# A four-layer trunk in split-float32 products: gate tiles and most of the conv input projection as seven half-width products per pair of weight tiles

## The chip, the cores and the metric

The kernel runs on one core of one Trainium2 chip. The metric is the device time of one execution in microseconds. One launch computes the whole network; the inputs come from HBM and the result goes back to HBM. The names of the engines are those of the profile: PE (TensorE) with its weight loads PEld, DVE (VectorE), ACT (ScalarE), POOL (GpSimd), SP (SyncE, which issues most DMAs).

## The reference

One sequence of 512 tokens with 1024 features goes through four layers, pool, conv, MLA, pool, and a last norm. Each layer is `x = x + mixer(rms_norm(x))`; everything is float32 and D_INNER is 2048. The pool mixer's `pooled` is the trailing mean over 2, 4, 8 or 16 tokens minus the token; MLA's `o` comes from 16 heads of causal softmax attention.

```python
def pool_mixer(xn, w_in, w_grp, scale, w_out):
    u, z = jnp.split(xn @ w_in, 2, axis=-1)            # 1024 -> 2 x 2048
    ...
    mixed = jnp.einsum('bsgc,gcd->bsgd', pooled, w_grp).reshape(B, S, D_INNER) * scale
    return (mixed * jax.nn.silu(z)) @ w_out            # 2048 -> 1024

def conv_mixer(xn, w_in, conv_w, w_out):
    b, c, h, z = jnp.split(xn @ w_in, 4, axis=-1)      # 1024 -> 4 x 2048
    y = b * causal_depthwise_conv(c * h, conv_w)       # width 3
    return (y * jax.nn.silu(z)) @ w_out

def mla_mixer(...):
    q_lat, kv_lat, k_rope, z = jnp.split(xn @ w_in, [384, 640, 704], axis=-1)   # z has 2048
    ...
    return (o.reshape(B, S, D_INNER) * jax.nn.silu(z)) @ w_out
```

## The kernel before

Activations lie feature-major: a tile is 128 features by 512 tokens, so `x` is 8 tiles and an inner activation is 16. Weights arrive from HBM in chunks of 128x1024 (512 KB): the 8 k-tiles of 128x128 that make one output tile of an input projection, or half of one of an output projection.

A float32 product is made of three faster products. Each operand is split into a high part (rounded, type fp32r) and a low part (the rest), and `mm3` (L156 to L159) adds high by high (L157), high by low (L158, here with the activation's low part) and low by high (L159). A weight chunk goes through `wchunk`: one DMA on SP, the high part `wh` on ACT (L152), the low part `wl` on DVE (L153). `mtile` runs the 8 k-tiles of one output tile through `mm3`: 24 matmuls of 128x512 into one PSUM bank. The activations are split once per layer (`xh` L230, `xl` L231), unnormed; the norm's factor of each token comes later (`Stats`, L175 to L218) and is multiplied into each output tile as `R`.

The stages in order of time are: pool layer 0 (to about 225 us of the profile), its output projection (to 315), the conv layer's input projection (to 690) and output projection (to 765), the MLA layer's input projection (to 885), its attention (to 1097), output projection (to 1185), pool layer 1 with its output projection and the closing norm (to 1505). In the input projections a `Layer` runs tile after tile. What is done with an output tile is its post: in pool, `post_u` scales it and makes sliding sums on POOL, `post_z` scales the gate tile (`sz`, L280) and applies SiLU; in conv, a channel tile takes four output tiles: c and h are multiplied (`post_c`, `post_h`), three taps make the convolution (L360 to L362), b is multiplied in on DVE and `R` on POOL (`post_b`, L366 and L367), and the gate z, then the product is split (`post_z`, L373 and L139); in MLA, sixteen gate tiles are among the first tiles' and the attention's work.

No order is written down for the engines, apart from a few `issue_after` hints: a scheduler places each instruction when its program is built, from its own estimates. Tiles of activations share one pool of 67 buffers, chunks have their own pools.

Of the kernel before, what the change touches and what calls it, by code (L numbers as in the profile page):

```python
# [33 lines left out]
CH = 1024  # L34
WARM = 8
# [7 lines left out]
# columns of the per-partition parameter array  # L43
# [11 lines left out]
# columns of the constant array  # L55
# [4 lines left out]
def trunk_kernel(ctx: ExitStack, tc: tile.TileContext, a):  # L60
    nc = tc.nc
    cp = ctx.enter_context(tc.tile_pool(name="cp", bufs=1))
    xp = ctx.enter_context(tc.tile_pool(name="xp", bufs=1))
    wp = ctx.enter_context(tc.tile_pool(name="wp", bufs=3))
    up = ctx.enter_context(tc.tile_pool(name="up", bufs=67))
# [11 lines left out]

    def ps(s):
        return pp.tile([P, S], F32, tag="ps", name=nm(s))
# [5 lines left out]
    con = cp.tile([P, NCON], F32, name="con")  # L85
    par = cp.tile([P, NPAR], F32, name="par")
    xt = [xp.tile([P, S], F32, name=f"x{m}") for m in range(KD)]
    dummy = cp.tile([P, S], F32R, name="dummy")
# [10 lines left out]

    raw0 = {}  # L100
# [4 lines left out]
    def load_w(m, hf):  # L105
        raw0[m, hf] = ut("wr")
        nc.sync.dma_start(raw0[m, hf], a["pool_in0"][m][:, hf * S : (hf + 1) * S])
# [11 lines left out]
    raw2 = []  # L119
    for m in (2, 3):  # L120
        raw2.append(wp.tile([P, CH], F32, tag="wr", name=nm("wr")))
        nc.sync.dma_start(raw2[-1], a["pool_in0"][m])
    nc.sync.dma_start(con, a["con"])
# [5 lines left out]
    def pcol(name, i):  # L129
        return par[:, PC[name][0] + i : PC[name][0] + i + 1]  # L130

# [10 lines left out]
    def wchunk(src, width=CH, pool=False, raw=None):  # L142
        if raw is None:
            raw = wp.tile([P, CH], F32, tag="wr", name=nm("wr"))[:, :width]
            nc.sync.dma_start(raw, src)
        h = wp.tile([P, CH], F32R, tag="wh", name=nm("wh"))[:, :width]
        l = wp.tile([P, CH], F32R, tag="wl", name=nm("wl"))[:, :width]
        if pool:
            nc.gpsimd.tensor_scalar(out=h, in0=raw, scalar1=1.0, scalar2=1.0, op0=ALU.mult, op1=ALU.mult)
            nc.gpsimd.tensor_tensor(out=l, in0=raw, in1=f(h), op=ALU.subtract)  # L150
        else:
            nc.scalar.activation(h, raw, AF.Copy)  # L152
            nc.vector.tensor_tensor(out=l, in0=raw, in1=f(h), op=ALU.subtract)  # L153
        return h, l
# [6 lines left out]
    def mtile(out, wh, wl, xs, k0=0, kn=KD, ktot=KD, stride=P, off=0):  # L161
        """out += sum over kn k-tiles of w[k].T @ xs[k0 + k]"""
        for k in range(kn):
            c = slice(k * stride + off, k * stride + off + P)
            mm3(out, wh[:, c], wl[:, c], *xs[k0 + k], first=(k0 + k == 0), last=(k0 + k == ktot - 1))

    class Stats:
        """sum of squares over the feature tiles, then the norm's factor of each token"""
# [4 lines left out]
        def add(self, t):  # L173
            sq = ut("sq")
            nc.scalar.activation(sq, t, AF.Square)  # L175
            if self.sum is None:
                self.sum = sq
            else:
                eng = nc.vector if self.i == self.n - 1 else nc.gpsimd
                eng.tensor_tensor(out=self.sum, in0=self.sum, in1=sq, op=ALU.add)  # L180
            self.i += 1
            if self.i == self.n:
                self.parts = split(self.sum, "ss")

        def rows(self):
            """the factor of token 128 i + p in column i of partition p"""
# [4 lines left out]
            for i in range(NT):  # L191
                d = sp.tile([P, P], F32, tag="sd", name=nm("sd"))
                nc.vector.tensor_tensor_reduce(
                    out=d, in0=st[:, i * P : (i + 1) * P], in1=ident, scale=1.0 / self.dim, scalar=EPS,
                    op0=ALU.mult, op1=ALU.add, accum_out=v[:, i : i + 1],
                )
            r = sp.tile([P, NT], F32, tag="sr", name=nm("sr"))
            nc.gpsimd.tensor_tensor(out=r, in0=v, in1=mhalf, op=ALU.pow)
            return r

        def start(self):
            r = self.rows()
# [18 lines left out]
    class XNorm:  # L221
        """xg = x * gain, split, with the statistics of x"""

        def __init__(self, gain):
            self.gain, self.xs, self.st = gain, [], Stats(D, KD)

        def add(self, m, stats=True):
            g = pcol(self.gain, m)
            h, l = ut("xh", F32R), ut("xl", F32R)
            nc.scalar.activation(h, xt[m], AF.Identity, scale=g)  # L230
            nc.vector.scalar_tensor_tensor(out=l, in0=xt[m], scalar=g, in1=f(h), op0=ALU.mult, op1=ALU.subtract)  # L231
            self.xs.append((h, l))
            if stats:
                self.st.add(xt[m])

    class Layer:
        """A layer's first tiles wait in PSUM until the norm's factor is there."""

        def __init__(self, xn, at=(1, 3)):
            self.xn, self.R, self.n, self.posts, self.at = xn, None, 0, [], at  # L240

        def tile(self, src, what, post, pt=None, raw=None):
            if pt is None:
                wh, wl = wchunk(src, raw=raw)
                pt = ps(what)
                mtile(pt, wh, wl, self.xn.xs)
            self.n += 1
            if self.n == self.at[0]:
                self.xn.st.start()
            self.posts.append((post, pt))  # L250
            if self.n == self.at[1]:
                self.R = self.xn.st.bcast()
            if self.R is not None:
                for fn, t in self.posts:
                    fn(t)
                self.posts = []

    def out_half(w, ys, m, hf, o, pool=False, after=()):
        with ExitStack() as es:
            for i in after:  # L260
                es.enter_context(tc.issue_after(i))
            wh, wl = wchunk(w[m, hf], pool=pool)
        mtile(o, wh, wl, ys, k0=8 * hf, kn=8, ktot=KI)

    def out_proj(w, ys, gain, o0=None, after=()):
        """x += y @ w, feature-major; the next layer's XNorm (o0: the first half of its first tile)"""
        xn = XNorm(gain)
        for m in range(KD):
            if m == 0 and o0 is not None:
                o = o0  # L270
            else:
                o = ps("o")
                out_half(w, ys, m, 0, o, after=after if m < 2 else ())
            out_half(w, ys, m, 1, o, pool=m == 0 and o0 is not None)
            nc.vector.tensor_tensor(out=xt[m], in0=o, in1=xt[m], op=ALU.add)
            xn.add(m)
        return xn
# [5 lines left out]
    def pool_layer(j, xn, mid=None, pre=(), at=(1, 3)):  # L283
        win, wg = a[f"pool_in{j}"], a[f"pool_grp{j}"]
        ys = []
        ly = Layer(xn, at)
        pre, later = list(pre), []
        for g, w in enumerate(WINDOWS):
            pooled, szs = [], []

            def post_u(pu):
                u = up.tile([P, S + PAD], F32, tag="u", name=nm("u"))
                nc.gpsimd.memset(u[:, :PAD], 0.0)
                tmul(u[:, PAD:], pu, ly.R)
                cur, d = u, 1
                while d < w:
                    nx = up.tile([P, S + PAD], F32, tag="u", name=nm("s"))
                    lo = 2 * d - 1
                    nc.gpsimd.tensor_tensor(out=nx[:, lo:], in0=cur[:, lo:], in1=cur[:, lo - d : S + PAD - d], op=ALU.add)  # L299
                    cur, d = nx, 2 * d  # L300
                pd = ut("pd")
                nc.vector.scalar_tensor_tensor(out=pd, in0=cur[:, PAD:], scalar=1.0 / w, in1=u[:, PAD:], op0=ALU.mult, op1=ALU.subtract)
                hd = sp.tile([P, PAD], F32, tag="hd", name=nm("hd"))
                nc.vector.tensor_tensor(out=hd, in0=cur[:, PAD : 2 * PAD], in1=con[:, C_INV + PAD * g : C_INV + PAD * (g + 1)], op=ALU.mult)
                nc.vector.tensor_tensor(out=pd[:, :PAD], in0=hd, in1=u[:, PAD : 2 * PAD], op=ALU.subtract)
                pooled.append(split(pd, "pl"))

            def post_z(pz):
                sz = ut("sz")
                tmul(sz, pz, ly.R)  # L310
                nc.scalar.activation(sz, sz, AF.Silu)
                szs.append(sz)

            def mix(g=g, pooled=pooled, szs=szs):
                for mm in range(2):
                    wh, wl = wchunk(wg[g, mm])
                    for e in range(2):
                        i = 2 * mm + e
                        pm = ps("pm")
                        mtile(pm, wh, wl, pooled, kn=4, ktot=4, stride=2 * P, off=e * P)  # L320
                        y = ut("y")
                        nc.vector.scalar_tensor_tensor(out=y, in0=pm, scalar=pcol(f"pool_scale{j}", 4 * g + i), in1=szs[i], op0=ALU.mult, op1=ALU.mult)
                        ys.append(split(y, "y"))
# [505 lines left out]
```

## Time and profile before

| | |
|---|---|
| median of 3 runs | 1505.94 us (1505.82 to 2998.67) |
| profiled execution: span, first to last instruction | 1504.8 us, 17426 instructions |
| PE busy | 99% of the span, 6712 matmuls |
| DVE, ACT, POOL busy | 52%, 33%, 20% |
| granted TensorE clock, mean | 0.995 |
| DMA | 140.5 MB, mean 93 GB/s |

The profile's only time for its own execution is the span; the two undisturbed runs lie 1.0 and 1.1 us above it. Busy times are sums of the durations of instructions. Matmuls are pipelined: the duration shown for a 128x512 matmul is about 390 ns, while the next one starts much sooner, so how fast PE goes is read from the distance of starts, not from durations. The idle time in a row of a group of instructions is that of the engine just before them, with what ended it.

### The profile page before, as it was taken

Reading aid. Unit: us, or ns where it says so; the run is one execution under the profiler, and the core shown is the slowest. Engines: PE = TensorE matmul, PEld = TensorE weight load, DVE = VectorE, ACT = ScalarE, POOL = GpSimd, SP = SyncE. Lnnn points to the kernel's source line nnn. Section 1 sums busy time; section 2 is a strip of 40 time slices with the busy share of each in tenths; the row PEclk is TensorE's granted clock in tenths of the full one; section 3 lists DMA queues with packets and bytes.
Section 4 is the critical chain, followed back from the end, with each engine's and each line's share of the span. In section 5 each row is a group of like instructions: output and inputs, shape, how many; then the busy total and the mean of one; then the engine's idle time right before and its main releaser. Section 6 shows DMA issues by size and latency. Waiting matters only on the chain.

```text
span 1504.8 us, 17426 instructions
## 1 busy us (share of the span) xinstructions
PE 1490.4 (99%) x6712; PEld 1221.1 (81%) x6712; DVE 779.5 (52%) x1250; ACT 495.0 (33%) x772; POOL 305.2 (20%) x312
## 2 busy tenths in 40 slices
PE   9999999999999999999999999899999999999998
PEld 7888888888888888888888878788888888888887
DVE  4665454335554555556345545666643455545442
ACT  5333233322222222223232424445632233333331
POOL 2223320111000000000101035445711111134010
PEclk9999999999999999999999999999999999999999
DMA  6233323233333333333233232223123333323331
GB/s 214 85 98 98 98 93 92 96 97 95 90 96 98 99 86 97 98 98 98 88 95 105 82 94 69 67 75 81 43 85 98 91 92 98 88 95 99 100 111 56
DMA packets 42659, 140.49 MB, mean 93 GB/s; under 512 B 5584, under 2 KB 5584, under 8 KB 42576
## 3 DMA queue, kind: packets, MB, share of 16 engines
q1 hardware_dynamic: 41712, 137.81, 30.3%
q10 hardware_dynamic: 864, 1.57, 0.3%
q8 instruction: 52, 0.85, 0.2%
q14 instruction: 31, 0.25, 0.1%
HBM read 132.80 MB, written 2.10 MB: 90 GB/s over the span
## 4 chain that ended last, share of the span: by engine, by line
PE 97%; DVE 1%; issue 0%; ACT 0%; DMA 0%; SPq 0%; POOLq 0%; POOL 0%; ACTq 0%
PE pz L159 8%; PE pz L157 8%; PE pz L158 8%; PE o L157 6%; PE o L158 6%; PE o L159 6%; PE pu L159 4%; PE pu L157 4%; PE pu L158 4%; PE pb L159 2%; PE pc L159 2%; PE ph L159 2%; PE pm L158 2%; PE pm L159 2%; PE pm L157 2%; PE ph L157 2%
## 5 line engine op out<-in xcount | busy, mean ns | idle before, releaser
L152 ACT ACTIVATE wh<-wr 128x1024 fp32r<-128x1024 f32 x222 | 235.4, 1060 | 699.7 <-issue 183.1
L153 DVE TENSOR_TENSOR wl<-wr,wh 128x1024 fp32r<-128x1024 f32 x222 | 298.5, 1345 | 226.3 <-ACT wh L152 226.1
L159 PE MATMUL pz<-xh,wl 128*128 128x512 f32 x512 | 201.8, 394 | 0.3 <-DVE wl L153 0.3
L157 PE MATMUL pz<-xh,wh 128*128 128x512 f32 x512 | 201.5, 394 | 0.0
L158 PE MATMUL pz<-xl,wh 128*128 128x512 f32 x512 | 200.9, 392 | 0.0
L157 PE MATMUL o<-yh,wh 128*128 128x512 f32 x384 | 151.4, 394 | 0.0
L159 PE MATMUL o<-yh,wl 128*128 128x512 f32 x384 | 151.2, 394 | 0.0
L158 PE MATMUL o<-yl,wh 128*128 128x512 f32 x384 | 151.1, 393 | 0.0
L159 PEld LDWEIGHTS pz<-xh,wl 128*128 128x128 f32 x512 | 96.1, 188 | 22.9 <-DVE wl L153 0.7
L158 PEld LDWEIGHTS pz<-xl,wh 128*128 128x128 f32 x512 | 96.3, 188 | 22.5
L157 PEld LDWEIGHTS pz<-xh,wh 128*128 128x128 f32 x512 | 96.1, 188 | 21.9
L159 PE MATMUL pu<-xh,wl 128*128 128x512 f32 x255 | 100.6, 396 | 0.3 <-DVE wl L630 0.3
L157 PE MATMUL pu<-xh,wh 128*128 128x512 f32 x255 | 100.6, 399 | 0.0
L158 PE MATMUL pu<-xl,wh 128*128 128x512 f32 x255 | 100.5, 395 | 0.0
L180 POOL TENSOR_TENSOR sq<-sq,sq 128x512 f32<-128x512 f32 x25 | 42.0, 1681 | 264.6 <-ACT sq L175 264.2
L299 POOL TENSOR_TENSOR s<-u 128x527 f32<-128x527 f32 x32 | 37.4, 1169 | 267.8 <-DVE u L280 247.3
L280 DVE TENSOR_TENSOR sz<-pz,R 128x512 f32<-128x512 f32 x64 | 42.4, 687 | 87.7 <-PE pz L159 87.7
L159 PEld LDWEIGHTS o<-yh,wl 128*128 128x128 f32 x384 | 72.2, 188 | 16.7
L158 PEld LDWEIGHTS o<-yl,wh 128*128 128x128 f32 x384 | 72.2, 188 | 16.5
L157 PEld LDWEIGHTS o<-yh,wh 128*128 128x128 f32 x384 | 72.2, 188 | 16.4
L367 POOL TENSOR_TENSOR yb<-yb,R 128x512 f32<-128x512 f32 x16 | 20.7, 1293 | 309.9 <-DVE yb L366 309.9
L299 POOL TENSOR_TENSOR s<-s 128x525 f32<-128x525 f32 (+2 forms) x48 | 63.9, 1331 | 3.8
(229 smaller groups left out, 2839.8 us busy)
## 6 DMA issues: line engine op xcount, KB each, us to landing
wr<-in_conv_in SPq DMA_DIRECT2D x64, 512.0 KB, 3.6
wr<-in_pool_in SPq DMA_DIRECT2D x62, 512.0 KB, 3.7
wr<-in_pool_out SPq DMA_DIRECT2D x32, 512.0 KB, 3.7
wr<-in_mla_in SPq DMA_DIRECT2D x22, 512.0 KB, 3.6
wr<-in_pool_grp SPq DMA_DIRECT2D x16, 512.0 KB, 3.6
wr<-in_conv_out SPq DMA_DIRECT2D x16, 512.0 KB, 3.7
wr<-in_mla_out SPq DMA_DIRECT2D x16, 512.0 KB, 3.7
wr<-in_q_up SPq DMA_DIRECT2D x12, 384.0 KB, 3.1
```

Source lines behind the costliest of these rows:

```text
L152: nc.scalar.activation(h, raw, AF.Copy)
L153: nc.vector.tensor_tensor(out=l, in0=raw, in1=f(h), op=ALU.subtract)
L157: nc.tensor.matmul(out, ah, bh, start=first, stop=False)
L158: nc.tensor.matmul(out, ah, bl, start=False, stop=False)
L159: nc.tensor.matmul(out, al, bh, start=False, stop=last)
L180: eng.tensor_tensor(out=self.sum, in0=self.sum, in1=sq, op=ALU.add)
L280: nc.vector.tensor_tensor(out=dst, in0=src, in1=R, op=ALU.mult)
L299: nc.gpsimd.tensor_tensor(out=nx[:, lo:], in0=cur[:, lo:], in1=cur[:, lo - d : S + PAD - d], op=ALU.add)
L367: nc.gpsimd.tensor_tensor(out=y, in0=y, in1=ly.R, op=ALU.mult)
```

## The change

Fifty-four pairs of output tiles are no longer computed as 2 x 24 matmuls of 128x512: all 16 gate tiles of both pool layers and of MLA (8 pairs each), and of the conv layer everything but the first channel tile, as pairs (c, h) and (b, z) of the channel tiles 1 to 15 (30 pairs). The two tiles (call them E and O), the even and odd k-tiles of the contraction, and the two halves of the 512 tokens make a 2x2 by 2x2 block product, which Strassen's scheme in Winograd's form does with seven block products instead of eight. Each of the seven (`product`) is 4 k-tiles x 3 = 12 matmuls of 128x256, so a pair takes 84 of these.

The weight forms are made per pair from three stored blocks (`load_pair`, `prepare_pair`): `r` holds A22 and A11, `r4` holds A12, and `s13` gets S1 and S3 by loading the same 256 KB block into both halves and then adding `r`'s source on top with an accumulating DMA, which is issued from POOL. S2 and S4 are two additions on DVE. Each form is split as before: `high` is a copy on ACT (L390), `low` a subtraction on DVE (L393). Of the activations, sums and differences of halves are made and split once per layer (`forms`). `seven` runs the products in the order A11, S1, A22, A12, S2, S4, S3; partial sums are copied out of PSUM by ACT (`snap`, into the single buffer `kept`), and two additions on DVE make E and O. O comes with a negative sign, which its post takes off with a negated `R`.

```python
def load_pair(src):                                                        # new
    r, r4, s13 = wt("wr", "wr", F32), wp.tile([P, S], F32, tag="wq", ..., bufs=2), wt("s13", "wr", F32)
    nc.sync.dma_start(r, src[:, :CH])                                      # L116
    nc.sync.dma_start(r4, src[:, CH + S :])
    for q in range(2):
        nc.sync.dma_start(s13[:, q * S : (q + 1) * S], src[:, CH : CH + S])
    nc.gpsimd.dma_start(s13, src[:, :CH], accum_op=ALU.add)                # L120

def prepare_pair(raw):                                                     # new
    ...
    def sums():
        nc.vector.tensor_tensor(out=r[:, S:], in0=s13[:, :S], in1=r[:, S:], op=ALU.add)
        nc.vector.tensor_tensor(out=r4, in0=r[:, S:], in1=r4, op=ALU.add)
    ...
    return w, {4: [high(r, ah)], 5: [low(r, ah, al), high(r4, ch)],
               6: [low(r4, ch, cl), sums, high(s13, sh)],
               7: [low(s13, sh, sl), high(r[:, S:], th[:, :S]), high(r4, th[:, S:])],
               9: [low(r[:, S:], th[:, :S], tl[:, :S]), low(r4, th[:, S:], tl[:, S:])]}

def seven(w, xf, now):                                                     # new
    ...
    now(0); p = product(w, xf, "A11", "B12", X, begin=True)
    now(1); q = product(w, xf, "S1", "N1", V, begin=True);   snap(part(0), V)
    now(2); product(w, xf, "A22", "T4", Y, after=p);         snap(part(2, 2), bx)
    now(3); product(w, xf, "A12", "B22", Z, after=q)
    now(4); product(w, xf, "S2", "N2", X);                   snap(part(1), X)
    now(5); product(w, xf, "S4", "B21", V, end=True)
    now(6); product(w, xf, "S3", "T3", X, end=True)
    nc.vector.tensor_tensor(out=E, in0=bv, in1=part(1, 2), op=ALU.add)     # L456
    nc.vector.tensor_tensor(out=halves(O), in0=twice(X), in1=kept...[:, ::3], op=ALU.add)   # L457
    now(7)

class Stream:                                                              # new
    def step(self):
        j = self.at; self.at += 1
        self.load(j + 1); self.load(j + 2)
        now, self.later = self.later, Steps()
        now.put(self.prepare(j + 1))
        self.jobs[j][2](self.ready.pop(j, None), now)
        now(7)
        ...

# conv layer
-            ly.tile(win[KI + i], "pc", post_c)
-            ly.tile(win[2 * KI + i], "ph", post_h)
-            ly.tile(win[i], "pb", post_b)
-            ly.tile(win[3 * KI + i], "pz", post_z)
+            else:
+                ly.pair(stream, a["conv_in"][2 * i - 2], (post_c, post_h))
+                ly.pair(stream, a["conv_in"][2 * i - 1], (post_b, post_z))
```

All of this runs as jobs of a `Stream`. A job has positions 0 to 7, between its products or k-tiles; the next job's weights are prepared at fixed positions of the job that runs, and posts follow at fixed positions of the next; a position over 7 is that position minus 8 in the following job. From the first pool layer to the MLA input projection the program order of PE, DVE and ACT is the order in which this code is written; in pool layer 1 the scheduler still places most of it.

Smaller edits go with it: in conv the first tap moves from DVE to ACT, the factor `R` of the b tile goes into the factors of the others and POOL's multiplication (L367) goes; the output projections of pool layer 0 and conv are split into two passes over `x`, so DVE adds to `x` 16 times more, and in conv scales each of 16 half sums by `R` first; the activations' pool grows to 70 buffers, the weight pools shrink to 4 raw, 6 split and 2 half-size buffers.

Per program, on PE 128x512 matmuls fall from 6040 to 3472 and 128x256 ones rise from 224 to 4712. On DVE 128x512 TENSOR_TENSOR instructions rise from 429 to 881, and 64 SCALAR_TENSOR_TENSORs of 128x256 are new. On ACT, 128x512 instructions rise from 372 to 640, 128x256 ones from 34 to 158. There are 54 accumulating DMAs on POOL's queue.

The order on DVE in the middle of conv, before. Each row is one instruction, output left of the arrow; `wl` is the low part of a weight chunk, and L280, L357, L360 to L362, L366, L373 and L139 are posts.

```order
L366 TENSOR_TENSOR yb_3005<-pb_2980,cv_2970 128x512 [waits DVE_49,PE_49]
L153 TENSOR_TENSOR wl_3083<-wr_3080,wh_3082 128x1024 [waits DMAHW6_49,Activation_49]
L280 TENSOR_TENSOR sz_3039<-pz_3014,R_2560 128x512 [waits PE_49]
L153 TENSOR_TENSOR wl_3121<-wr_3118,wh_3120 128x1024 [waits DMAHW7_49,Activation_49]
L373 TENSOR_TENSOR yb_3005<-yb_3005,sz_3039 128x512 [waits Activation_49,Pool_49]
```

Between two chunks' low parts stand one or two posts of tiles that PE has finished. The same place in the change, for one pair (the next pair's forms `al`, `cl`, sums, `sl`, around E and O of the pair that runs on PE; L714 is a post):

```order
L393 TENSOR_TENSOR al_4672<-wr_4534,ah_4671 128x1024 [waits DMAHW1_49,Activation_49]
L393 TENSOR_TENSOR cl_4674<-wq_4535,ch_4673 128x512 [waits DMAHW4_49,Activation_49]
L396 TENSOR_TENSOR wr_4534<-s_813_4536,wr_4534 128x512 [waits DMAHW2_49,DMASW4_49,DVE_49]
L397 TENSOR_TENSOR wq_4535<-wr_4534,wq_4535 128x512 [waits DVE_49]
L456 TENSOR_TENSOR E_4681<-bv_4680,kept_4683 128x512 [waits PE_49]
L457 TENSOR_TENSOR O_4682<-bx_4679,kept_4683 128x512 [waits PE_49]
L393 TENSOR_TENSOR sl_4676<-s_813_4536,sh_4675 128x1024 [waits DMAHW3_49,Activation_49]
L714 TENSOR_TENSOR cv_4662<-E_4681,cv_4662 128x512 [waits DVE_49]
```

The low part of S1 and S3 (`sl`) of the next pair now stands behind E and O of the running pair, and these stand behind `cl` and the two sums. On ACT, in the same pair, `kept` being the copies out of PSUM:

```order
L437 ACTIVATE kept_4683<-bv_4680 128x256 [waits DVE_49,PE_49,Activation_49]
L437 ACTIVATE kept_4683<-bx_4679 128x512 [waits PE_49]
L705 ACTIVATE cv_4662<-ch_4661,par 128x512 [waits DVE_49,Pool_49]
L390 ACTIVATE ah_4671<-wr_4534 128x1024 [waits DMAHW1_49]
L437 ACTIVATE kept_4683<-bx_4679 128x256 [waits PE_49]
L390 ACTIVATE ch_4673<-wq_4535 128x512 [waits DMAHW4_49]
L390 ACTIVATE sh_4675<-s_813_4536 128x1024 [waits DMAHW3_49,DMAHW2_49,DMASW4_49]
```

`ch`, which `cl` on DVE needs, stands behind the third copy, which waits for the running pair's fifth product S2; `sh` needs the accumulating DMA (DMASW). On PE, of one pair's first two products, these rows stand where the second one begins; `sh` and `sl` are the split S1:

```order
L417 MATMUL bv_4680<-fh_2752,sh_4546 128x256 [waits PE_49,Activation_49]
L422 MATMUL bv_4680<-fl_2753,sh_4546 128x256
L423 MATMUL bv_4680<-fh_2752,sl_4547 128x256 [waits DVE_49]
```

The third matmul of the second product waits for DVE's `sl`; before, PE's tile waited at its third matmul for a `wl` in the same way.

More of the change, by code (lines that the diff above doesn't have):

```diff
@@ L253, in tile @@
             if self.R is not None:
-                for fn, t in self.posts:
-                    fn(t)
+                for n, (fn, t, sign) in enumerate(self.posts):
+                    stream.later.put(fn(t, sign), 0 if len(self.posts) < 3 else n * self.gap)
                 self.posts = []
[L258 to L263, printed above, removed]
```

814 lines of the change are left out of this document (558 added, 256 removed).

## The prediction

> **What bounds the kernel now.** First the page's head, the busy time of each engine, and the chain that ended last.
>
> ```profile
> span 1504.8 us, 17426 instructions
> PE 1490.4 (99%) x6712; PEld 1221.1 (81%) x6712; DVE 779.5 (52%) x1250; ACT 495.0 (33%) x772; POOL 305.2 (20%) x312
> PE 97%; DVE 1%; issue 0%; ACT 0%; DMA 0%; SPq 0%; POOLq 0%; POOL 0%; ACTq 0%
> core 0: 1504.8 us, clock 0.995
> ```
>
> PE runs without a gap at the full clock, and the chain is PE for 97%. DVE has half its time free. So fewer PE cycles are worth their time, as long as nothing else becomes late. Next the groups that feed PE, and two stretches: conv's input projection, and the start, where DMA is busiest.
>
> ```profile
> L159 PE MATMUL pz<-xh,wl 128*128 128x512 f32 x512 | 201.8, 394 | 0.3 <-DVE wl L153 0.3
> L153 DVE TENSOR_TENSOR wl<-wr,wh 128x1024 fp32r<-128x1024 f32 x222 | 298.5, 1345 | 226.3 <-ACT wh L152 226.1
> L153 DVE TENSOR_TENSOR wl<-wr,wh x222: 1211/1226/2305, 15.8 to 1462.0; 128x1024 fp32r<-128x1024 f32 x111
> 0.00:30.00 30.00, 27.38 (x99) 20.55 (x100) 15.74 (x23) 17.09 (x26) 9.41 (x14) 0.94 0.71 234
> 320.00:690.00 370.00, 370.00 (x1604) 300.88 (x1603) 203.19 (x246) 93.24 (x105) 23.57 (x34) 1.00 0.31 94
> ```
>
> PE lost 0.3 us to late low parts in 512 matmuls, so the preparation runs well ahead. In conv, DVE works 203 of 370 us. The L153 row without an arrowed idle time gives its shortest, median and longest duration: 1.21, 1.23 and 2.31 us.
>
> **Term 1: PE's stream.** Spacing is read from starts. The end of the trace has both widths of the same instruction in one run of matmuls: 28 steps from the first to the second row, 29 from the third to the fourth.
>
> ```profile
> 1485.76 0.39 PE L158 MATMUL po<-wl,yh 128*128 128x512 f32 x1
> ...
> 1492.24 0.39 PE L159 MATMUL po<-wh,yl 128*128 128x512 f32 x1
> 1492.47 0.28 PE L157 MATMUL po<-wh,yh 128*128 128x256 f32 x1
> ...
> 1495.89 0.28 PE L159 MATMUL po<-wh,yl 128*128 128x256 f32 x1
> ...
> 1000.20 0.28 PE L535 MATMUL s<-kl,qh 128*128 128x128 f32 x1
> ...
> 1000.54 0.28 PE L538 MATMUL s<-krl,qrs 128*128 128x128 f32 x1
> ```
>
> That is 0.2314 us at 512 columns and 0.1179 at 256. Two tiles cost 48 x 0.2314 = 11.11 us, a pair of seven products 84 x 0.1179 = 9.90. The gain is 1.20 us a pair, **65 us** for 54 pairs. At 128 columns the spacing is still 0.113 (three steps), so half width stands just above a floor and nothing smaller would help.
>
> Here the Trainium skill speaks against the change: its page "TensorE: Matmul & The Clock Gate", section "Back-to-back issue gap", says that in a stream of weight loads and matmuls the spacing is set by both, 81 ns at 128 columns and 131 ns at 512. Halving the width then saves far less than half; between these figures 256 columns would cost an estimated 98 ns, three quarters of the full width. The trace disagrees: 0.1179 is 0.51 of 0.2314.
>
> **Term 2: a new loop through three engines.** Before, the low part of a chunk had a tile's time of slack. Now DVE's order is fixed: the next pair's `al`, `cl`, two sums, then E and O of the running pair, then the next pair's `sl`. E and O wait for PE's last products; `cl` waits for ACT's `ch`, which stands behind the third copy out of PSUM, which waits for PE's S2; and PE's second product needs `sl` at its third matmul. Handoffs and spacings are in these rows.
>
> ```profile
> 401.53 0.74 DVE L361 SCALAR_TENSOR_TENSOR cv<-ch,par,cv 128x512 f32<-128x512 f32 x1
> 402.31 0.75 DVE L362 SCALAR_TENSOR_TENSOR cv<-ch,par,cv 128x512 f32<-128x512 f32 x1
> 404.31 0.39 PE L159 MATMUL pb<-xh,wl 128*128 128x512 f32 x1
> 404.74 0.69 DVE L366 TENSOR_TENSOR yb<-pb,cv 128x512 f32<-128x512 f32 x1 [1.68 <-PE pb L159]
> 404.56 1.06 ACT L152 ACTIVATE wh<-wr 128x1024 fp32r<-128x1024 f32 x1 [4.48 <-PE pb L158]
> 405.65 2.23 DVE L153 TENSOR_TENSOR wl<-wr,wh 128x1024 fp32r<-128x1024 f32 x1 [0.22 <-ACT wh L152]
> 410.05 1.06 ACT L152 ACTIVATE wh<-wr 128x1024 fp32r<-128x1024 f32 x1 [4.43 <-PE pz L158]
> 411.01 0.62 ACT L372 ACTIVATE sz<-sz 128x512 f32<-128x512 f32 x1
> 894.54 0.69 DVE L139 TENSOR_TENSOR qal<-t,qah 128x512 fp32r<-128x512 f32 x1
> 895.15 0.68 DVE L503 TENSOR_TENSOR t<-t,qr 128x512 f32<-128x512 f32 x1
> 897.48 1.23 DVE L153 TENSOR_TENSOR wl<-wr,wh 128x1024 fp32r<-128x1024 f32 x1 [0.26 <-ACT wh L152]
> 898.76 0.50 PE L159 MATMUL pz<-xh,wl 128*128 128x512 f32 x1 [0.31 <-DVE wl L153]
> L563 ACT ACTIVATE th<-pj 128x256 fp32r<-128x256 f32 x16 | 6.6, 414 | 0.0
> L136 ACT ACTIVATE yh<-yb 128x512 fp32r<-128x512 f32 x16 | 10.1, 631 | 20.4 <-DVE yb L373 20.4
> L139 DVE TENSOR_TENSOR yl<-yb,yh 128x512 fp32r<-128x512 f32 x16 | 11.1, 692 | 10.5 <-ACT yh L136 10.5
> ```
>
> PE to DVE and ACT to DVE take 0.03 us beyond the end of the first. On DVE a dependent instruction starts 0.04 after the one before, an independent one 0.08 before its end (each costs 0.61); on ACT an independent one 0.10 before (411.01 against 411.11). From the end of `wl` (898.71) PE restarts at 898.76 with a matmul 0.11 longer than usual, so 0.16 in effect.
>
> Take t = 0 where a pair's `sl` ends. PE resumes at 0.16 and issues S1's last ten matmuls to 1.34, A22 to 2.75, A12 to 4.17; the last matmul of S2 starts at 5.46 and ends at 5.74. ACT copies 256 columns from 5.77 to 6.18, then `ch` from 6.08 to 6.71. DVE: `cl` 6.74 to 7.43, the first sum to 8.04, the second, which depends on it, to 8.77. PE finished S4 at 7.16 and S3 at 8.58, so E and O don't wait: E to 9.38, O to 9.99. The next `sl`, 1.23 long, ends at **11.14**. PE reached the matmul that needs it at 8.58 + 14 x 0.1179 = 10.23 and stands still. A pair behind a pair costs about 11.15 us, 1.25 more than its matmuls, and 0.04 more than the two old tiles. All of the other preparation fits in between: from 0 to 6.7 DVE has `al`, two low halves and at most four posts, 1.2 + 1.2 + 2.8 = 5.2.
>
> How many pairs stand behind a pair? Conv has two unbroken runs of 14 and 16 pairs (channel tiles 1 to 7 and 8 to 15, with an output pass between): 28 pairs behind another; MLA's eight give 7; in the pool layers the gates stand in twos, 4 each. That is 43. **43 x 1.25 = 54 us given back**. The other 11 keep their gain. Of what the loop takes, each duration could come out up to 0.1 shorter in nine steps, or the longest `wl` (2.31) could stand in for 1.23: 43 x -0.9 and 43 x +1.1 give bounds of -39 and +47 us.
>
> **What else is added or moved.** In the places where the new order puts rare work ahead of a pair, I price by these rows.
>
> ```profile
> L198 POOL TENSOR_TENSOR sr<-sv,mhalf 128x4 f32<-128x4 f32 x6 | 8.9, 1478 | 88.0 <-DVE sv L193 88.0
> L193 DVE CUSTOM_DVE_ANT_0 sd<-st,con 128x128 f32<-128x128 f32 x24 | 5.5, 287 | 10.7 <-PE st L189 10.7
> L210 DVE TENSOR_SCALAR dg<-con,rh 128x128 fp32r<-128x128 f32 x24 | 5.2, 281 | 0.0
> L280 DVE TENSOR_TENSOR sz<-pz,R 128x512 f32<-128x512 f32 x64 | 42.4, 687 | 87.7 <-PE pz L159 87.7
> wr<-in_conv_in SPq DMA_DIRECT2D x64, 512.0 KB, 3.6
> ```
>
> A norm's factor takes four reductions, a power on POOL and eight scalings on DVE: 4 x 0.29 + 1.48 + 8 x 0.28 = 4.9 us, about 3 of them behind PE's running job. Where they stand in front of a pair's `al` or `sl`, PE waits: I put 3 us for pool layer 0's first gate pair, 3 for the starts of conv and MLA together, 7 in MLA (the latents' norms and the rotary key stand among the gate pairs: one full factor of 4 and some 1 us elsewhere), and 3 for the first mix, where six tiles' posts of 0.69 wait at once. In pool layer 1 the scheduler may put `sl` ahead of E; for its four pairs I take back 4. Sum **+12**, bounds 0 (all covered) and +25 (doubled).
>
> The output projections' 16 more additions and 16 scalings, at 0.69, lie beside 32 half tiles of 5.55 us of PE (24 x 0.2314) each and cost nothing; without that cover they would be 22 us. The activations' sums (64 of 256 columns) come in output passes whose DVE is idle likewise. POOL loses its multiplication beside conv's `wl`, which took 2.23 there (405.65), and the freed time is off the path.
>
> The accumulating DMA isn't in the trace. In a run of pairs its target's two plain loads can start at t = 3.2, when the half-size low parts have freed the buffer, and land 3.6 later, at 6.8; `sh` and the first sum need the result one job later, at 17.8 to 18.0. So it has 11 us. A plain load of the same size takes 3.6; moving three times the bytes (read twice, written once) makes about 7 at most by my estimate (2 x 3.6). Both fit, so I cost it at nothing. Traffic is no bound: 1.75 MB read a pair in 11.15 us is 157 GB/s, against 234 GB/s at a share of 0.71 in the first 30 us.
>
> Sum: 1504.8 - 65 + 54 + 12 = 1506 span; the median of the shown runs lies 1.1 above its span, so 1507. I say **1507 us**: no change.
>
> **The rivals.** (A) *The loop has slack.* PE's queue is deep and all handoffs were read off the tightest rows; if the loop closes under 9.9 us (E and O faster, or `ch` early), PE's 65 us stay, less 0 to 30: 1441 to 1475, faster. For it: DVE is free for 167 of 370 us in conv. Against it: the free time does not help what is in order. (B) *The accumulating DMA lands late*, slower: it is issued on POOL's queue after the plain loads have landed, and `sh`, the sums, E, O and `sl` all wait behind it on DVE. It decides from 11 us after its target's loads; at 13 us each of 43 pairs gains 1.7 more, +73: 1580. For it: no row shows an accumulate. Against it: 11 us is three plain loads. (C) *DVE becomes the bound*: two conv pairs are 20.2 us of DVE work by durations (20 instructions at 0.69, two at 0.75, four at 1.23), more than two pairs' PE time of 19.8; with 1.345, the mean of `wl`, a cycle is 20.7, still below 2 x 11.15 = 22.3, but with waits in between a pair may come to 11.5: 43 x 0.35 = +15, 1522, no change. (D) *The half-width product doesn't pay*: at three quarters of a full one, 0.174, a pair costs 14.6 and the kernel 1504.8 + 54 x 3.5 = 1694. The 30 half-width starts above speak against it. That is what the skill's rule named above would give.
>
> **How the numbers follow.** My forecast has 0.45, within 1478 to 1536; A 0.30; B 0.14; C 0.10; D 0.01. What a measurement of this kernel can tell from no change is 2%, 30 us. A lies wholly on the faster side; of the forecast's own spread 0.02 is put on either side. Faster 0.30, same 0.54, slower 0.16. The range reaches into A and to the upper bounds of the terms: 1455 to 1550; it leaves out the lower part of A (0.12) and the most of B (0.08).
>
> **What would show it.** In the new trace, matmuls of 256 columns at 0.118 us; in conv, PE idle some 0.9 to 1.3 us in each pair at the second product's third matmul, released by DVE `sl`; `ch` ahead of which ACT waits for PE; a pair period of 11.1 to 11.2; DVE over 85% busy there. If the period is 9.9, A holds; if DVE waits for a DMA ahead of the first sum, B; if DVE never waits, C. I am wrong if the fixed order lets `sl` end before PE has reached its third matmul.

## The result, and the profile after

The changed kernel takes 1594.41 us (median of 4 runs, 1591.97 to 1595.59), against 1506.05 us before: a ratio of 1.0585, interval 1.0569 to 1.0600. One of the four runs before took 2998.67 us; the ratio leaves it out. The change is 88 us slower; 1507 us was forecast, in a range from 1455 to 1550. The page's head and the clock of the profiled execution:

```profile
span 1591.7 us, 22646 instructions
PE 1469.5 (92%) x8632; PEld 1285.6 (81%) x8632; DVE 1095.4 (69%) x1753; ACT 684.6 (43%) x1166; POOL 335.2 (21%) x345
PE 29%; DVE 5%; issue 2%; POOL 2%; ACT 1%; DMA 1%; SPq 0%; POOLq 0%; ACTq 0%
core 0: 1591.7 us, clock 0.979
```

PE is no longer busy all the time, and the granted clock has fallen from 0.995 to 0.979. To see where, I took each matmul's distance to the start of the next and set beside it the full-clock distance of its width (0.2314 us for 512 columns, 0.175 for 384, 0.1179 for 256, 0.113 for 128). An excess over 0.2 us counts as a stall, the small rest as slowed matmuls.

| us | before | after | difference | forecast |
|---|---|---|---|---|
| stream of matmuls at full clock | 1482.6 | 1417.5 | -65.1 | -65 |
| stalls for `sl` (the pair's loop) | 0 | 55.4 | +55.4 | +54 |
| all other stalls | 10.1 | 80.7 | +70.6 | +12 |
| slowed matmuls | 4.0 | 29.6 | +25.6 | none |
| ahead of the first and behind the last | 8.1 | 8.5 | +0.4 | none |
| span | 1504.8 | 1591.7 | +86.9 | +1 |

The same by stages, from PE's first matmul of one to the first of the next (each stage with its output projection, the attention counted from its first scores), with the experiments told below:

| us | pool 0 | conv | MLA input | attention | pool 1 | span |
|---|---|---|---|---|---|---|
| before | 320.7 | 444.4 | 138.8 | 278.3 | 322.5 | 1504.8 |
| the change | 354.5 | 459.3 | 159.5 | 288.1 | 330.3 | 1591.7 |
| early low part | 351.3 | 432.5 | 149.3 | 287.2 | 327.2 | 1547.5 |
| scheduler's order | 332.3 | 482.3 | 165.9 | 290.0 | 320.0 | 1590.6 |
| written order, full width | 335.1 | 455.8 | 143.4 | 288.2 | 325.8 | 1548.3 |
| early low part and three edits | 333.7 | 416.2 | 148.1 | 288.8 | 325.1 | 1512.0 |
| the same, pairs in conv alone | 324.8 | 415.4 | 142.7 | 289.8 | 327.1 | 1499.8 |
| and the last gate as filler | 327.8 | 414.8 | 138.7 | 286.4 | 325.5 | 1493.1 |

The loop is where the prediction put it. One period of it on DVE, in the middle of conv:

```profile
642.37 1.22 DVE L393 TENSOR_TENSOR sl<-s,sh 128x1024 fp32r<-128x1024 f32 x1
...
650.36 0.69 DVE L393 TENSOR_TENSOR cl<-wq,ch 128x512 fp32r<-128x512 f32 x1
...
652.29 0.68 DVE L456 TENSOR_TENSOR E<-bv,kept 128x512 f32<-128x512 f32 x1
652.89 0.68 DVE L457 TENSOR_TENSOR O<-bx,kept 128x512 f32<-128x512 f32 x1
653.49 1.22 DVE L393 TENSOR_TENSOR sl<-s,sh 128x1024 fp32r<-128x1024 f32 x1
```

From one `sl` to the next are 11.12 us (forecast 11.14; over conv's two runs of pairs, by PE's starts, 10.95 to 11.13); counted from the end of the first at 643.59, `cl` starts at 6.77 (forecast 6.74). PE, at the matmul that needs `sl`, and the list of what PE waited for, with us in total, times and the longest:

```profile
653.54 0.28 PE L422 MATMUL bv<-fl,sh 128*128 128x256 f32 x1
654.76 0.39 PE L423 MATMUL bv<-fh,sl 128*128 128x256 f32 x1 [0.94 <-DVE sl L393]
PE bv L423 <- DVE sl L393: 48.4, 42, 3.7
PE s L921 <- ACT kh L158: 15.0, 2, 10.2
PE o L257 <- ACT wh L244: 11.7, 4, 6.3
PE bv L417 <- ACT kept L437: 6.3, 3, 4.7
PE pt L257 <- ACT wh L244: 5.2, 3, 3.1
PE o L259 <- DVE wl L247: 4.9, 6, 2.6
PE pj L948 <- POOL p L935: 4.4, 4, 1.9
```

By spacing, conv has 28 such stalls of 1.05 to 1.15 us, 30.4 in all (28 x 1.25 = 35 were forecast; about 0.1 us of each pair's loss comes right behind the stall and stands in the row of slowed matmuls). The other 15, in the pool layers, MLA and at conv's start, are 0.2 to 3.9 us long and make up 25.0 (15 x 1.25 = 19 were forecast).

The rest was not forecast. One case is the rotary tables, on DVE and ACT, and PE's next chunk:

```profile
545.00 0.42 DVE L747 CAST t<-posi 128x512 f32<-128x512 int32 x1
...
553.70 0.69 DVE L769 TENSOR_TENSOR t<-t,ang 128x512 f32<-128x512 f32 x1
553.24 0.63 ACT L765 ACTIVATE sin<-ang 128x512 f32<-128x512 f32 x1 [14.76 <-DVE ang L764]
555.06 2.93 ACT L244 ACTIVATE wh<-wr 128x1024 fp32r<-128x1024 f32 x3
549.50 0.39 PE L259 MATMUL o<-yh,wl 128*128 128x512 f32 x1
556.15 0.80 PE L257 MATMUL o<-yh,wh 128*128 128x512 f32 x1 [6.26 <-ACT wh L244]
556.74 0.63 PE L258 MATMUL o<-yl,wh 128*128 128x512 f32 x1
```

Sixteen instructions, nearly all dependent on one another, run for 9.4 us on DVE; ACT waits for them at `sin`, the next chunk's `wh` is written behind `sin` and `cos`, and PE stands still for 6.3 us. Then the first two matmuls start 0.59 us apart, not 0.23. The clock, in the window's column PEclk (the third figure from the end of a row):

```profile
538.00:575.00 37.00, 30.70 (x122) 23.96 (x121) 21.69 (x32) 6.80 (x8) 0.88 (x1) 0.91 0.24 71
640.00:720.00 80.00, 73.60 (x611) 72.09 (x610) 68.06 (x96) 42.85 (x70) 7.51 (x12) 1.00 0.64 162
955.00:985.00 30.00, 19.83 (x90) 16.41 (x89) 19.07 (x31) 10.07 (x22) 12.41 (x10) 0.83 0.29 79
```

Conv's regular stalls of 1.1 us leave the clock at 1.00 (the second row), the long ones of the other two rows do not.

In pool layer 0 the mean of a sliding sum is written on DVE at a fixed place, and DVE waits there for POOL, with the next weights' low parts behind:

```profile
156.42 0.18 DVE L613 TENSOR_TENSOR hd<-s,con 128x16 f32<-128x16 f32 x1 [8.88 <-POOL u L600]
266.20 0.18 DVE L613 TENSOR_TENSOR hd<-s,con 128x16 f32<-128x16 f32 x1 [7.29 <-POOL u L600]
DVE hd L613 <- POOL u L600: 29.1, 6, 8.9
DVE hd L613 <- POOL s L606: 8.1, 6, 3.4
```

### The profile page after: what moved, and what is told of

Read it like the earlier page. It is cut to its first block, busy times and chain, and to the rows that moved or that the text cites. A ratio compares the mean times of both kernels' runs of the same rounds, so it can differ in the third digit from the quotient of the medians.

```text
span 1591.7 us, 22646 instructions
## 1 busy us (share of the span) xinstructions
PE 1469.5 (92%) x8632; PEld 1285.6 (81%) x8632; DVE 1095.4 (69%) x1753; ACT 684.6 (43%) x1166; POOL 335.2 (21%) x345
## 5 line engine op out<-in xcount | busy, mean ns | idle before, releaser
L247 DVE TENSOR_TENSOR wl<-wr,wh 128x1024 fp32r<-128x1024 f32 x116 | 148.7, 1284 | 51.8 <-ACT wh L244 51.7
L244 ACT ACTIVATE wh<-wr 128x1024 fp32r<-128x1024 f32 x116 | 120.9, 1051 | 130.9 <-PE o L258 50.1
L257 PE MATMUL pt<-xh,wh 128*128 128x512 f32 x335 | 133.6, 399 | 5.9 <-ACT wh L244 5.2
L259 PE MATMUL pt<-xh,wl 128*128 128x512 f32 x335 | 133.3, 398 | 2.4 <-DVE wl L247 2.4
L258 PE MATMUL pt<-xl,wh 128*128 128x512 f32 x335 | 132.7, 396 | 0.7 <-DVE xl L346 0.7
L423 PE MATMUL bv<-fh,sl 128*128 128x256 f32 x216 | 66.1, 306 | 48.4 <-DVE sl L393 48.4
L257 PEld LDWEIGHTS o<-yh,wh 128*128 128x128 f32 x384 | 73.1, 190 | 29.6 <-ACT wh L244 13.4
L393 DVE TENSOR_TENSOR al<-wr,ah 128x1024 fp32r<-128x1024 f32 x54 | 68.5, 1269 | 36.7 <-ACT ah L390 36.7
L257 PEld LDWEIGHTS pt<-xh,wh 128*128 128x128 f32 x335 | 63.6, 190 | 21.6 <-ACT wh L244 6.3
L259 PEld LDWEIGHTS pt<-xh,wl 128*128 128x128 f32 x335 | 63.4, 189 | 20.2 <-DVE wl L247 5.7
L258 PEld LDWEIGHTS pt<-xl,wh 128*128 128x128 f32 x335 | 63.5, 189 | 15.1 <-DVE xl L346 1.0
```

The lines of the kernel that those rows point to most:

```text
L247: (nc.gpsimd if pool else nc.vector).tensor_tensor(out=l, in0=raw, in1=f(h), op=ALU.subtract)
L257: nc.tensor.matmul(out, ah, bh, start=first, stop=False)
L258: nc.tensor.matmul(out, ah, bl, start=False, stop=False)
L259: nc.tensor.matmul(out, al, bh, start=False, stop=last)
L393: return lambda: nc.vector.tensor_tensor(out=l, in0=t, in1=f(h), op=ALU.subtract)
L423: nc.tensor.matmul(out, wl[:, c], xh, start=False, stop=end and kk == KK - 1, skip_group_check=True)
```

## The experiments

**The loop: `sl` ahead of E and O.** In `prepare_pair`:

```
-   6: [low(r4, ch, cl), sums, high(s13, sh)],
-   7: [low(s13, sh, sl), high(r[:, S:], th[:, :S]), ...
+   6: [low(r4, ch, cl), high(s13, sh), sums, low(s13, sh, sl)],
+   7: [high(r[:, S:], th[:, :S]), ...
```

> The low part of S1 and S3 is made ahead of E and O on DVE, and nothing else moves. Theory (the loop of term 2, read with the new trace: a pair behind a pair takes 11.1 us): the low part then ends about 1.2 us earlier in the loop, at 9.9 instead of 11.1 us, PE reaches the matmul that needs it at 10.2, so the wait of 1.07 to 1.14 us in 28 conv pairs goes, and in some ten pairs elsewhere: 40 us less than 1594, about 1553 (1545 to 1560), and a pair behind a pair in conv takes 9.9 to 10.1 us. Rival (DVE is the bound, its order only decides who waits): the pair stays at 10.6 or more, and 15 us at most are gained.

Measured: 1549.64 us, 45 less than the change; against the kernel before 1.0289 (1.0272 to 1.0306). Conv falls from 459.3 to 432.5, below the 444.4 of before. In the list of PE's waits:

```profile
PE bv L423 <- DVE sl L393: 17.6, 14, 3.3
```

The loop and its price are shown: one instruction moved, 45 us. Of the stalls for `sl`, 55.4 us by spacing, 20.1 stay, most of them in the pool layers and MLA. Conv's second run of pairs takes 163 us for 16, 10.2 each, a little over the 9.9 to 10.1 expected: four waits of 0.6 to 1.2 us are left.

**The order left to the scheduler.** `tc.manual_schedule` is taken away around the stream.

> The same products, forms and jobs, but the program order of PE, DVE and ACT is left to the scheduler everywhere, as it was before the change. Theory (the written order costs the time: stalls of PE of 126 us more than before, and 26 us of lowered clock behind them): most of it goes, 1455 to 1490 us, with PE waiting less than 40 us in all. Rival (seven products need more preparation than the engines can give in time, in any order): conv's pairs stay at 10.8 us or more and the time over 1540.

Measured: 1592.27 us, ratio 1.0571 (1.0555 to 1.0587). The theory is wrong. The rival's numbers are met (over 1540 us, conv's pairs at 13.2 us in the first run and 11.1 in the second), but its "in any order" is not: written orders below prepare conv's pairs in about 10 us. Pool layer 0 gains 22 us against the change, so there the written order does cost time; conv loses 23, and there it is another chain. DVE and POOL in the first half of conv, and two rows of what DVE waited for in all:

```profile
484.36 0.87 POOL L120 DMA_DIRECT2D s<-in_conv_in  x1 [12.50 <-DMA s<-in_conv_in]
484.97 0.69 DVE L392 TENSOR_TENSOR cl<-wq,ch 128x512 fp32r<-128x512 f32 x1
492.14 0.69 DVE L395 TENSOR_TENSOR wr<-s,wr 128x512 f32<-128x512 f32 x1 [6.48 <-issue]
DVE wr L395 <- issue: 37.6, 8, 6.9
DVE wr L395 <- DMA s<-in_conv_in: 22.3, 4, 6.7
```

POOL waits for the target's plain loads, issues the accumulating DMA at 484.36, and DVE's first sum, its first user, starts at 492.14, 6.9 us after the issue has ended. The profile names no releaser for this wait ("issue"), but the instruction has to wait for that DMA, and four others like it are put down to it. Here the accumulate is late, as rival (B) had it, but in an order that the change does not use.

**The written order with full-width tiles.** Each pair becomes two plain tiles; forms, sums and copies are left out. The sign that the c x h factor has for pairs is not taken back; this changes values and no work.

```
-   def run(w, now):
-       E, O = seven(w, self.xn.fm, now)
-       self.done(stream, (post[0], E, 1), (post[1], O, -1))
-       ...
+   self.tile(stream, src[0], post[0])
+   self.tile(stream, src[1], post[1], then)
```

> The written order is kept, but each pair is computed as two tiles of 24 matmuls of 128x512 as before the change; the forms, sums and copies of the pairs are left out. Theory (two separate losses, the pair's loop and the written order): no loop, but the waits at the layers' borders, at the rotary tables and in the pool layers stay, some 50 to 70 us with the clock behind them: 1550 to 1580. Rival (the waits come from the pairs' preparation alone): within 10 of 1506.

Measured: 1550.13 us (one run), at the low end of the theory. With the old products the rest of the change, the written order and the smaller edits together, still costs 43 us: 14 in pool 0, 11 in conv (6.5 of them the rotary tables' stall), 5 in MLA's input, 10 in the attention, 3 in pool 1.

**No accumulating DMA.**

```
-   nc.gpsimd.dma_start(s13, src[:, :CH], accum_op=ALU.add)
    ...
+   4: [high(r, ah), lambda: nc.vector.tensor_tensor(out=s13, in0=r, in1=s13, op=ALU.add)],
```

> The accumulating DMA on POOL's queue is replaced by an addition of 128x1024 on DVE, early in each job. Theory (the accumulate lands in time, 6.1 us after issue, but holds POOL's queue while its target's loads are under way, and in pool layer 0 the sliding sums stand behind it): conv's pairs stay at 11.1 to 11.3 us, pool layer 0 gains 5 to 10 us, 1580 to 1595 in all. Rival (the accumulate is what is late): conv's pairs fall to 10 us, 40 us gained. Third case (DVE has no room for 1.2 us more): pairs of 11.6 or more, 1605 or more.

Measured: 1616.17 us (one run), the third case: conv's stalls become 1.3 and 2.3 us in turn, and `sl` costs PE 70.5 us.

```profile
PE bv L422 <- DVE sl L392: 70.5, 44, 3.7
L403 DVE TENSOR_TENSOR s<-wr,s 128x1024 f32<-128x1024 f32 x54 | 67.1, 1243 | 14.5 <-DMA s<-in_pool_z 14.5
```

DVE has no 1.24 us to spare in a pair. By itself this run does not clear the accumulate, since it puts work on the loop in its place; that the accumulate was no cause of conv's loss follows from the change's own trace, where nothing on DVE or ACT in conv's pairs waits for it, and from the 45 us that the early low part gave back with the accumulate left as it was. Pool 0 gained 4.6 us, less than forecast.

**Three places where the order blocks,** each on top of the early low part (1549.6), then all together. The tables:

```
-   ts(out=n0, in0=ang, ...)
+   ops.append(lambda: ts(out=n0, in0=ang, ...))
...
+   for n, op in enumerate(ops):
+       s1.later.put({2 * n + 4: [op]})
```

> On top of the kernel with the early low part (1549.6 us): the rotary tables' 17 instructions on DVE and 2 on ACT, written in one piece in conv's first output pass, are spread, one in every second position of the following jobs. Theory (they stand in front of the next weight chunk on both engines; PE waited 6.4 us there, and the clock was at half for 6.8 us behind it): 9 to 11 us less, about 1540. Rival (the wait moves to the next late chunk): less than 3 us.

Measured: 1542.04 us (one run), 7.6 less, a little under the theory; conv 423.0 against 432.5. The chunks:

```
-   return (h, l), {1: [high], 2: [low]}
+   return (h, l), {-1: [high], -0.5: [low]}
```

> On top of the kernel with the early low part (1549.6 us): in each job the next plain chunk's high part goes ahead of everything else on ACT, its low part ahead of the activations' split on DVE. Theory (in the output passes the chunk's high part stands behind the split of the x tile that PE has just finished, so each wait goes round PE, DVE, ACT, DVE and PE): the waits of 0.5 to 2.8 us for chunks at the passes' ends go, 8 to 15 us less, 1535 to 1542. Rival (DVE has no room left in these passes, and only what comes first changes): less than 3 us.

Measured: 1541.96 us (one run), 7.7 less, a little under the theory: 4 in conv, 3 in pool 0. The means (group 0 as it was):

```
-   return {0: [mul], 8: [mean], 11: [high], 13: [low]}
+   return {0: [mul], 14: [mean], 17: [high], 19: [low]} if g else {...}
```

> On top of the kernel with the early low part (1549.6 us): in the pool layers the means of groups 1 to 3, which wait on DVE for POOL's sliding sums, are written six positions later. Theory (DVE stood still for 37 us at these, with the next weights' low parts behind): 5 to 15 us less, 1535 to 1545, most of it in pool layer 0. Rival (POOL's sums are late in any order, since they share POOL's queue with the accumulating DMAs): DVE's idle time there stays over 25 us and the time within 4 us.

Measured: 1539.4 us (one run), 10.2 less, all of it in pool 0 (339.7 against 351.3); DVE's waits at the means fall from 36.6 to 10.2 us. All three:

> The early low part, the spread tables, the chunks first and the late means together. If the waits are separate, their gains add: 22 to 40 us less than 1549.6, 1510 to 1528, still above the kernel before. If they cover one another (one engine is short of time), less than 15 us in all.

Measured: 1515.17 us, ratio 1.0060 (1.0043 to 1.0077), 34.5 less, where the three sum to 25.5. They do not cover one another; why together they are worth more was not tried.

**Where pairs pay.** On top of all this, gate tiles go back to full width, conv keeps its pairs:

> Pairs in conv alone; the gate tiles of pool and MLA are full-width tiles again, in the written order, with the early low part, the spread tables, the chunks first and the late means. By stages: conv as in the kernel with all four edits (416 us, against 444 before the change), pool layer 0 322 to 328 (full-width tiles in the written order had 335 without the late means and the chunks first), MLA's input 141 to 144, attention 288, pool layer 1 325: 1494 to 1502, 0.5% below the kernel before. Theory (short runs of pairs between other work lose more than their 1.2 us each, long runs gain): this is 10 to 18 us faster than with all pairs (1515). Rival (a pair is worth its 1.2 us anywhere): 24 gates' worth slower, over 1525.

Measured: 1502.93 us, ratio 0.9980 (0.9971 to 0.9990): 12 less than with all pairs, and 1 us above the range expected. At full clock PE's stream grows by 28.9 us (1446.4 against 1417.5), and its stalls and slowed matmuls fall by 41 (85.9 to 44.9). Pool 0 gains 9 us and MLA's input 5 by giving up 16 pairs; pool 1 loses 2. Next the gate tiles as filler ahead of the attention:

> As the kernel with pairs in conv alone, and the last four gate tiles of MLA are left to the scheduler, which may put them between the first tiles of the attention. Theory (PE waits 9 and 5 us for the first heads' high parts because the gate tiles, which stood there before the change, now end in a block ahead of it): the first wait falls below 2 us with the clock behind it, 5 to 12 us less. Rival (the wait is the length of the chain from the rotary parts to the first head and has no filler): within 3 us.

Measured: 1501.41 us, ratio 0.9969 (0.9958 to 0.9979), 1.5 less: the wait stayed at 4.65 us. That is the rival's number, but not for its reason: the scheduler left the tiles where they were written, so there was still no filler. Writing the last one behind `stage_a(0)` by hand:

> As the kernel with pairs in conv alone (1502.9 us); MLA's last gate tile is written behind the first head's query and key projections, where it stood before the change. Theory (PE waits 4.65 us for the first head's high part because nothing is written between its projections and its scores): the wait falls below 1 us and the half clock behind it goes, 4 to 8 us less, 1495 to 1499, about 0.6% below the kernel before. Rival (the chain from the rotary parts is as long as the tile): within 2 us.

Measured: 1496.15 us, ratio 0.9929 (0.9916 to 0.9943), 6.8 less; the wait at the first head falls to 0.62 us. This version is 0.7% below the kernel before, little but clear of the interval, and 6% below the change: PE is busy again.

```profile
span 1493.1 us, 20243 instructions
PE 1463.7 (98%) x7768; PEld 1249.5 (84%) x7768; DVE 943.0 (63%) x1513; ACT 597.7 (40%) x986; POOL 310.1 (21%) x321
350.00:480.00 130.00, 129.59 (x1086) 128.60 (x1085) 120.84 (x170) 75.64 (x123) 11.19 (x19) 1.00 0.70 179
core 0: 1493.1 us, clock 0.993
```

The third row is the first half of conv: PE has no gaps, and DVE is busy for 120.8 of 130 us, so DVE would probably be next.

**The accumulate's target loaded first,** with all pairs:

> As the kernel with all four edits and all pairs (1515 us); each pair's loads into the accumulate's target are issued ahead of the other two loads. Theory (POOL's queue stands still until these loads have landed, and the sliding sums of the pool layer stand behind it; PE lost 6.35 us at one such place and the clock behind it): POOL's idle time for its target falls, pool layer 0 from 333.7 to 324 to 330 us, 1504 to 1512 in all. Rival (POOL's own work is what is late there): within 3 us.

Measured: 1510.39 us (one run), 4.8 less than the 1515.17 of all pairs and inside the range expected, but not where it was expected: pool 0 stayed at 334.3 (its stall of 6.35 us fell to 4.35, others grew), conv went from 416.2 to 412.4, its pairs from 10.1 to 10.0 and 9.9 us. So POOL's standing still for the loads is not shown to be what pool 0 loses. That in conv, with the loop cut, the accumulate's landing is close to the path would fit, but one run does not show it.

## Why the prediction was wrong

**Right: PE's stream, and the loop in conv.** -65 was measured as -65.1, the loop's period as 11.12 us against 11.14, and moving one instruction out of it gave 45 us back. The rule set against the change there, from the Trainium skill's page "TensorE: Matmul & The Clock Gate", section "Back-to-back issue gap" (by the prediction's estimate from it, three quarters of the price for half the width), was rightly given little: the trace after shows 256 columns 0.118 us apart.

**Partly luck: +54 for the loop, measured as +55.4.** Conv's 28 stalls came out 5 us under their 35, the other 15 came out 6 us over their 19. Six of these, of 1.5 to 3.9 us in pool layer 0 and MLA, are still there, at 1.6 to 3.5 us, when `sl` stands ahead of E and O; they are not the loop. Only 35 of the 55.4 us go with the loop.

**Wrong: the term "what else is added or moved", +12, measured as +96** (70.6 of stalls and 25.6 of slowed matmuls), beyond its bound of +25. It alone takes the sum from 1506 to 1590. Three steps of it failed.

First, the list was too short. It priced rare work ahead of pairs: a norm's factor, the first mix. It did not ask, for every long piece of work, what is written behind it on its engine. The rotary tables (6.4 us of stall), the pool means (10 us when moved) and the missing filler before the attention (6.8 us when put back) are not in it at all. MLA's input was given 7 us, with its eight pairs and their loop at -1; it lost 21 by stage.

Second, the output passes were costed at nothing, with 5.55 us of PE beside each half tile as cover. The cover was there in amount and not in order: a chunk's high part stood on ACT behind the split of the x tile that PE had only just finished, so a tile could pay the way round PE, DVE, ACT and back. One such place, in conv's last output pass:

```profile
784.42 0.69 DVE L530 TENSOR_TENSOR x<-xs,x 128x512 f32<-128x512 f32 x1
785.14 0.72 ACT L345 ACTIVATE xh<-x,par 128x512 fp32r<-128x512 f32 x1 [2.08 <-DVE x L530]
785.77 1.04 ACT L244 ACTIVATE wh<-wr 128x1024 fp32r<-128x1024 f32 x1
```

ACT stands idle for 2.08 us until `x` is there, though `wh` needs nothing of it, and PE goes on at 786.86, when `wh` is written, after a stall of 1.7 us. Putting chunks first took such stalls out of conv's passes and gave 7.7 us.

Third, the half clock behind a stall, which has no term in the prediction. Of the 25.6 us of slowed matmuls, 17 lie in stretches of half clock; most of the rest is a first matmul behind a stall. The prediction showed a window at 0.94 (0 to 30 us) and made nothing of it, and the trace before has a second one, around PE's one long wait:

```profile
PE s L534 <- ACT kh L136: 4.9, 1, 4.9
900.00:950.00 50.00, 45.04 (x228) 37.77 (x227) 33.09 (x74) 20.98 (x53) 25.33 (x24) 0.94 0.25 67
```

Some slips in its working change nothing. PE reaches the matmul that needs `sl` 84 spacings after it went on, at 10.07 and not at 10.23, which gives the 1.25 of the sum. A pair's loads are 1792 KB, 1.84 MB, so 165 GB/s and not 157. Less 30 us, (A) ends at 1471 and not at 1475, and the chances add up to 0.32, 0.51 and 0.17, not to 0.30, 0.54 and 0.16.

**The rivals.** (A) did not happen. (B), the late accumulate, had its sign right, and its 1580 lies near the result by luck; its mechanism is wrong: the accumulate landed in 6.1 us, inside its 11, and conv's loop ran without a wait for it.

```profile
s<-in_conv_in POOLq DMA_DIRECT2D x30, 512.0 KB, 6.1
```

(C), DVE as the bound, is not seen: with the loop cut, conv's pairs take 10.2 us, and 10.0 in the last versions, where DVE is busy for 93% of the time and PE has no gaps.

The attention's +9 to +12 us, in every version without the filler, is explained by it only in part (3.4 us by stage); a second wait of 5 us for a high part stands before and after, and 4 us of waits for POOL's probabilities were not there before. One thing in the trace of the change bears on it. Ahead of the first head three products on DVE, from 959.32 to 966.41, run beside the low parts of weights that POOL makes there (L247) and take 7.25 us; alone they take 0.69 each. In the kernel before, one instruction was slowed like this ahead of the first head, at 890.34.

```profile
959.32 2.89 DVE L885 TENSOR_TENSOR t<-qr,cos 128x512 f32<-128x512 f32 x1
958.95 2.71 POOL L247 TENSOR_TENSOR wl<-wr,wh 128x1024 fp32r<-128x1024 f32 x1
```

So up to 5 of the first wait's 10.3 us could come from there. No run moved POOL's work away, and this part stays open.

## What to carry to other kernels

A written order turns every instruction with a long wait into a wait of all that stands behind it on its engine: go through each engine's queue and ask of every slow or waiting piece what is behind it, not how much free time the engine has. A loop between engines can be added up from spacings in the trace, here to better than 0.1 us, and then it shows which instruction to move. A scheme that saves PE little per pair of tiles (1.2 us in 11) was worth it here in conv's long runs, where its preparation can run ahead, and not in the gate tiles' short runs of two and eight between other work (pool layer 1, at 2 us, aside).

## What the runs showed of the hardware

A long stall goes on costing time when it is over: in the trace's clock records of the changed kernel there are 13 stretches of half clock that begin during or within 2.1 us after stalls of 2.1 to 10.3 us, all 3.41, 6.83 or 10.24 us long, and one behind the last matmul. By the mean clock they take (1 - 0.979) x 1591.7 = 33 us, against 7.5 before (in part while PE stands still). Of single stalls between 2.1 and 2.9 us some drew a stretch (2.8 us at 163.8 and 875.1, 2.2 at 1557.5) and others none (2.8 at 901.0, 2.1 at 1068.6); conv's 28 stalls of 1.1 us, 11 us apart, drew none. The Trainium skill's page "TensorE: Matmul & The Clock Gate", section "What's actually happening", has a free-running window of about 3.4 us and two states; the lengths, multiples of 3.41, agree. The Trainium skill's rule on the same page, section "HAM oscillation — how this bites in real kernels", to have no idle gaps over about 3.4 us, is a little too wide for this kernel, where 2.2 us were enough in one place.

DVE's additions and subtractions with both inputs in SBUF were slowed beside POOL's sliding sums, mostly from 0.69 to 1.55 us for 128x512 and from 1.22 to 2.08 for 128x1024; with one input in PSUM (`u<-pt,R`) they kept 0.68 to 0.69 beside them. In pool layer 0 this hit ten instructions of the pairs' preparation, 7.5 us in all, while in conv, where POOL has little to do, every `al` and `sl` took 1.21 to 1.23.

```profile
268.07 1.60 DVE L621 TENSOR_TENSOR pll<-s,plh 128x512 fp32r<-128x512 f32 x1 [0.16 <-ACT plh L618]
269.60 2.08 DVE L393 TENSOR_TENSOR al<-wr,ah 128x1024 fp32r<-128x1024 f32 x1
268.06 1.07 POOL L606 TENSOR_TENSOR s<-u 128x527 f32<-128x527 f32 x1 [1.84 <-DVE u L577]
269.21 5.06 POOL L606 TENSOR_TENSOR s<-s 128x525 f32<-128x525 f32 x3
```
